# A gated linear attention block: the output gate's second half as two groups of 512 columns, three of its pair-steps by sums, and transposes and loads at later seams

## The chip, the cores and the metric

The kernel runs on one core of one Trainium2 chip. The metric is the device time of one execution in microseconds, as the median of several runs. PE is the matrix engine, DVE the vector engine, ACT the scalar engine, POOL the GpSimd engine and SP the engine that issues most DMAs. Every engine works through its own instructions in order.

## The reference

One layer: a chunked gated linear attention (GLA) with an output gate and an output projection, and an MLP with squared ReLU, each with RMSNorm ahead and a residual; 256 tokens of width 2048, in float32.

```python
def _gla_mixer(h, w_in, w_gate_up, b_gate, o_norm, w_out):
    proj = h @ w_in
    q, k, v, r, g_low = jnp.split(proj, [...], axis=-1)
    log_a = jax.nn.log_sigmoid((g_low @ w_gate_up + b_gate)) / GLA_GATE_TEMP
    ...
    _, o = lax.scan(step, s0, (qc, k_dec, vc, chunk_decay))
    o = o * lax.rsqrt(jnp.mean(o * o, axis=-1, keepdims=True) + EPS) * o_norm
    o = o.transpose(1, 0, 3, 2, 4).reshape(bsz, seq, GLA_VAL_WIDTH)
    return (o * jax.nn.silu(r)) @ w_out
...
    x = x + mixer(rmsnorm(x))
    x = x + (relu(rmsnorm(x) @ w_up) ** 2) @ w_down
```

The change touches the last part of the mixer: `r` (2048 columns of `proj`), its product with `o`, and the projection by `w_out` (2048 x 2048).

## The kernel before

Products are made in split float32: each factor is a high part (a cast to the matrix engine's rounded float32, on ACT) and a low part (the rest, on DVE), and three products of parts (high·high, high·low, low·high) stand for one. So each block of weights that arrives by DMA costs a cast on ACT (line 123) and a subtraction on DVE (line 136) before PE can use it.

The tokens are two row blocks of 128 (`NT`). The width is cut into 16 blocks of 128 rows of weights (kt), and in most places two of them make a pair-step (kp, 0 to 7) of 256 rows by 512 columns. `group` (line 294) runs eight such pair-steps for one group of 512 columns. A plain pair-step is 24 matmuls of 256 columns. A pair-step "by sums" (kp in `summed`) forms sums of blocks of weights and of inputs, as in Strassen's scheme, and needs 21: 9 in its own step and 12, `pending`, after the next step's matmuls. For that it loads its weights in two DMAs of 256 KB, adds one block onto another with an accumulating DMA that POOL issues (line 335) once the loads have landed, lets DVE make the sums (lines 233 and 234), and casts and splits a second slot (lines 363 and 365). After the last step by sums `combine` joins the sum banks.

Weights go through rings. `raw` has six buffers (and one "more"); the cast parts, `hi` and `lo`, have five slots, so the cast of the k-th slot waits until PE is done with the (k-5)th. A pair-step by sums takes two slots.

The order of the instructions on each engine is set by a scheduler that follows the program's order and its dependences; `tc.issue_after` puts an instruction behind another one in time, and `between[step]` runs side work (turns, loads, bank copies) at a seam, after the step's matmuls.

The stages around the change:

- `x_group(n, ...)` (line 731) runs `group` on columns of `w_in`: two groups of v (`V0`, `V1`), then two groups of r, the first half of the output gate (`G0`, `G1`), with the attention's heads (`attend`, line 781) at the seams. `gate_x` (line 801) takes Silu on ACT (line 803) and multiplies `on`, the attention's output, on DVE (line 804).
- The second half of the gate (1024 columns) goes through `natural` (line 183) instead: 16 steps of 128 rows by 1024 columns, 24 matmuls each, no sums. At its seams stand `side` jobs: after the third step turns 0 and 1, later four loads of `h` (the residual, `load_h`) and the copy of `h` into out group 0's banks (`begin_out(0)`). One job makes sums of `w_out` in advance and stores them (`make_sums`, lines 242 to 262). At the end `gate_out` (line 818) takes four Silus and four products.
- `turn` (line 839) transposes 512 columns of `on` on PE in 8 matmuls (line 845), and ACT and DVE put the result into `oth`/`otl` as high and low parts, or, for the kp in `FORMED`, as the input's sums (`turn_pair`, line 829, through the tiles `some` and `form`, lines 834 to 837). Turn q serves kp 2q and 2q+1.
- `out_group(g, ...)` (line 920) runs `group` on `w_out` for 512 output columns, g = 0 to 3, in the orders of `ORDER`. Turns 2 and 3 stand in out group 0 at step 1.

Of the kernel before, what the change touches and what calls it, by code (L numbers as in the profile page):

```python
# [29 lines left out]
AF = mybir.ActivationFunctionType  # L30
# [11 lines left out]
KEYW = HEADS * DK  # L42
# [27 lines left out]
def tile_gla_mlp(ctx, tc, x, xt, cols, w_vg, w_in, w_gate, w_out, w_up, w_down, final_norm, out):  # L70
# [14 lines left out]
    def psum_bank(i, name="acc"):  # L85
        return psum.tile([P, 512], F32, tag=f"b{i}", name=name)
# [21 lines left out]
    def flush():  # L108
        while side:
            side.popleft()()  # L110
# [272 lines left out]
    def rows(w, c0, n=G, r0=0):  # L383
        return lambda kt: w[r0 + kt * P : r0 + (kt + 1) * P, c0 : c0 + n]
# [122 lines left out]
    def load_h(t, half):  # L507
        h[t, half] = shared.tile([P, G], F32, tag=f"h{2 * half + t}", name="h")
        with tc.issue_after(last_load[0].ins):
            nc.sync.dma_start(out=h.get((t, half)), in_=x[t * P : (t + 1) * P, half * G : (half + 1) * G])  # L510
# [217 lines left out]
        scores(hd)  # L728
        scores(hd + 1, spare)

    def x_group(n, c0, order, summed, between, put, rows_of={}):

        def combine(p16, p57):
            tt = nc.vector.tensor_tensor
            nc.scalar.copy(comb_x[:, 1::2], two(p16))
            nc.scalar.copy(comb_x[:, 0::2], two(p57))
            tt(comb_x[:, 3], comb_x[:, 1], comb_x[:, 3], op=ALU.add)
            tt(comb_x[:, 0], comb_x[:, 0], comb_x[:, 3], op=ALU.subtract)
            tt(comb_x[:, 3], comb_x[:, 3], comb_x[:, 2], op=ALU.add)
            tt(comb_x[:, 2], comb_x[:, 0], comb_x[:, 2], op=ALU.subtract)  # L740

        def put_all(banks):
            for t in range(NT):
                o = comb_x[:, 2 * t : 2 * t + 2]
                nc.vector.tensor_tensor(o, two(banks[t]), o, op=ALU.add)
                put(o.rearrange("p f s -> p (f s)"), t)

        def at_of(kp):
            def at(k):
                if k < A12:  # L750
                    return [x_forms[kp][:, i, k] for i in range(2)]
                t, i = divmod((A11, A12, A21, A22).index(k), 2)
                return plain_x(2 * kp + i, t)
            return at

        def row(kt, t):
            return (row_x if (kt, t) in [(2 * kp + i, t) for kp in rows_of for t, i in rows_of[kp][:1]] else plain_x)(kt, t)

        group(
            lambda kp: w_in[2 * kp * P : 2 * (kp + 1) * P, c0 : c0 + GT], [psum_bank(i) for i in x_banks[n % 2]], x_sums,  # L760
            order, summed, between, row, at_of, combine, put_all, filled=False, rows_of=rows_of,
        )

    V0 = (5, 6, 2, 0, 7, 3, 4, 1), (0, 4)
# [41 lines left out]

    x_group(2, 4 * KEYW, *G0, {i + 1: f for i, f in enumerate(attends[:6])}, gate_x(0), {2: FIRST[2]})
    x_group(3, 4 * KEYW + GT, *G1, {i: f for i, f in enumerate(attends[6:])}, gate_x(GT), {2: FIRST[2]})
    acc_free.clear()
    acc_free.extend(x_banks[0] + x_sums + x_banks[1])  # L810
    jobs.extend(next(make))


    oth = otl = None

    some = mid.tile([P, 7, 512], F32, tag="qt", name="some")

    def gate_out(acc, c0):
        for c in range(2):
            for t in range(NT):  # L820
                lo = c0 + 512 * c
                s = some[:, 2 * c + t]
                nc.scalar.activation(s, acc[t][c], AF.Silu, scale=r1[:, t : t + 1])
                nc.vector.tensor_tensor(on[:, t, lo : lo + 512], on[:, t, lo : lo + 512], s, op=ALU.mult)

    FORMED = (0, 1, 6, 7)
    raw_forms = [in_forms(some[:, 4:6].rearrange("p a b -> p (a b)")), in_forms(mid.tile([P, G], F32, tag="db", name="form"))]
# [30 lines left out]
                nc.scalar.activation(dh, s, AF.Copy, scale=gain(kt))  # L858
                nc.vector.scalar_tensor_tensor(dl, s, gain(kt), dh.bitcast(F32), op0=ALU.mult, op1=ALU.subtract)

    once_x = lambda kt, t: (plain_x if kt == EVEN[1] else row_x)(kt, t)
    oth, otl = (big.tile([P, KT * T + 192], F32R, tag="B", name="ot" + i) for i in "hl")

    of_pairs = big.tile([P, 4 * G + 64], F32R, tag="C", name="of")[:, OFF:-16].rearrange("p (b i f s) -> p b i f s", b=2, i=2, f=8)
# [31 lines left out]
    def begin_out(g):  # L896

        for t in range(NT):
            out_banks[g, t] = bank = psum_bank(out_ids[2 * (g % 2) + t])
            nc.scalar.copy(bank, h[:, t, g * GT : (g + 1) * GT])  # L900

    def spare_out(g):
        return [psum_bank(out_ids[2 * (1 - g % 2) + t], "aux") for t in range(NT)]

    side.extend([nothing] * 2 + [lambda: (
        turn(on, turned_o, gain_o, 0, forms_o),
        turn(on, turned_o, gain_o, 1, forms_o, [psum_bank(i, "aux") for i in r_banks[4:]]),
    )])
    side.extend([nothing] + [lambda i=i: load_h(i % 2, i // 2) for i in range(4)] + [nothing] * 2 + [lambda: begin_out(0)])
    r_banks = list(acc_free)  # L910
    out_ids = r_banks[4:] + r_banks[:4]
    acc = natural(once_x, rows(w_in, 5 * KEYW), G, HALF, order=even_at(3, 5))
    flush()
    gate_out(acc, G)
    hs = const.tile([P, NT, 4], F32, name="hs")

    GROUPS = D // GT
# [27 lines left out]
    def ssq_h(g):  # L945
# [1 line left out]
            sq = tmp.tile([P, GT], F32, tag="t512", name="sq", bufs=1)  # L947
            nc.scalar.activation(sq, h[:, t, g * GT : (g + 1) * GT], AF.Square, accum_out=hs[:, t, g : g + 1])

    ORDER = (3, 0, 2, 1, 4, 7, 6, 5), (1, 3, 7, 2, 0, 6, 4, 5)  # L950
    newest[0] = None
    ordered[0] = True
    out_group(0, ORDER[0], FORMED, {
        1: lambda: (turn(on, turned_o, gain_o, 2), turn(on, turned_o, gain_o, 3, forms_o, spare_out(0))),
        3: lambda: begin_out(1),
    })
    hth, htl = (big.tile([P, KT, T], F32R, tag="A" + i, name="h" + i, bufs=1) for i in "hl")
    turned_h = lambda kt: [a[:, kt, :].rearrange("p (t s) -> p t s", t=NT) for a in (hth, htl)]
    for g in range(1, GROUPS):
        out_group(g, ORDER[1], FORMED if g == 3 else (0, 1, 7), {  # L960
            2: lambda: turn(h, turned_h, g2, g - 1), 4: lambda: ssq_h(g - 1),
            **({3: lambda: begin_out(g + 1)} if g + 1 < GROUPS else {}),
        })
# [511 lines left out]
```

## Time and profile before

| | |
|---|---|
| median of 3 runs | 1040.26 us (1039.97 to 1040.44) |
| the profiled execution | 1040.35 us |
| its span, first to last instruction | 1038.6 us |
| granted clock of PE | 0.998 |
| the second half of the gate, on PE | 238.78 to 284.12 us |
| turns 0 and 1 / turns 2 and 3, begin on PE | 246.94 us / 287.87 us |
| out group 0, begin on PE | 284.12 us |
| kp 7 of out group 0, begin on PE | 298.87 us |

Times count from the span's first instruction. In rows of the profile `L305` is line 305 of the program, `hi<-raw` is output from input by the tiles' names, `128x1024` partitions by elements, `x3` a count; a bracket holds the idle time of the engine ahead of the row and what ended it. A row of the timeline begins with start and duration, a row of the groups holds busy time and mean nanoseconds of one instruction behind the bar, then idle time by what ended it. A row of the chain begins with start and length. A row of the waits is waiter, releaser, total, count and longest.

### The profile page before, as it was taken

What the parts mean: (1) busy time and instruction counts of PE and PEld (TensorE: products, weight loads), DVE (VectorE), ACT (ScalarE), POOL (GpSimd) and SP (SyncE); (2) the same over time, 40 slices, a digit from 0 to 9 for tenths busy, and PEclk for the clock granted to TensorE, in tenths of its full rate; (3) what the DMA queues carried; (4) which work ended last, traced back from release to release, by engine and by line L of the source; (5) the groups of instructions that cost most, each with busy time, mean ns of one, the idle gap of its engine ahead of it and who ended that gap; (6) DMA issues with size and microseconds to landing.
All of it is one profiled execution on the core that took longest, in us unless ns stands there. A gap on an engine that the chain in (4) does not pass through costs nothing.

```text
span 1038.6 us, 23383 instructions
## 1 busy us (share of the span) xinstructions
PE 1029.9 (99%) x9016; PEld 1029.3 (99%) x9016; DVE 905.8 (87%) x1257; ACT 755.1 (73%) x1132; POOL 135.0 (13%) x181
## 2 busy tenths in 40 slices
PE   9999999999999999999999999999999999999997
PEld 9999999999999999999999999999999999999997
DVE  7769768898697876989999999999999999999987
ACT  7775556676576664678779788778778778778785
POOL 0000111310100001111111111111111111111100
PEclk9999999999999999999999999999999999999999
DMA  9967877758877877678888888887887888887872
GB/s 342 328 196 218 264 203 213 207 153 309 257 234 246 249 256 196 185 209 240 225 242 227 231 237 221 241 238 220 251 226 216 252 227 229 239 235 217 238 246 85
DMA packets 128751, 240.17 MB, mean 231 GB/s; under 512 B 11472, under 2 KB 30160, under 8 KB 128512
## 3 DMA queue, kind: packets, MB, share of 16 engines
q1 hardware_dynamic: 107472, 215.32, 65.8%
q0 software_dynamic: 20448, 21.77, 12.3%
q8 instruction: 70, 1.15, 0.4%
q10 hardware_dynamic: 720, 1.60, 0.4%
q14 instruction: 41, 0.34, 0.1%
HBM read 232.35 MB, written 6.29 MB: 230 GB/s over the span
## 4 chain that ended last, share of the span: by engine, by line
PE 98%; issue 0%; DMA 0%; ACT 0%; DVE 0%; POOLq 0%; POOL 0%; DVEq 0%; SPq 0%
PE up L1023 34%; PE acc L1023 28%; PE acc L305 16%; PE acc L181 10%; PE acc L224 6%; PE aux L224 2%; PE aux L181 1%; PE aux L845 1%; PE aux L696 1%; DMA raw<-in_w_vg 0%; ACT sqf L1362 0%; PE acc L595 0%; DVE hf L1434 0%; ACT hi L123 0%; POOLq L1471 0%
## 5 line engine op out<-in xcount | busy, mean ns | idle before, releaser
L123 ACT CAST hi<-raw 128x512 fp32r<-128x512 f32 (+4 forms) x656 | 519.0, 821 | 199.6 <-DVE raw L233 66.5
L136 DVE TENSOR_TENSOR lo<-raw,hi 128x768 fp32r<-128x768 f32 (+4 forms) x228 | 233.4, 1032 | 55.9 <-ACT hi L123 49.5
L1023 PE MATMUL acc<-hi,act 128*128 128x256 f32 x1694 | 247.6, 276 | 0.0
L1023 PE MATMUL up<-hh,hi 128*128 128x256 f32 x1024 | 238.7, 276 | 0.0
L1023 PE MATMUL up<-hl,hi 128*128 128x256 f32 x1024 | 238.7, 276 | 0.0
L1023 PEld LDWEIGHTS acc<-hi,act 128*128 128x128 f32 x1694 | 217.4, 188 | 0.0
L170 DVE TENSOR_TENSOR lo<-raw,hi 128x1024 fp32r<-128x1024 f32 x160 | 194.4, 1219 | 21.1 <-ACT hi L123 20.6
L1023 PEld LDWEIGHTS up<-hh,hi 128*128 128x128 f32 x1024 | 192.2, 188 | 0.0
L1023 PEld LDWEIGHTS up<-hl,hi 128*128 128x128 f32 x1024 | 192.2, 188 | 0.0
L1233 POOL DMA_DIRECT2D raw<-in_w_down x113 | 96.9, 857 | 518.1 <-DMA raw<-in_w_down 223.0
L1293 DVE TENSOR_TENSOR lo<-raw,hi 128x1024 fp32r<-128x1024 f32 x113 | 137.7, 1218 | 1.1 <-ACT hi L123 1.1
L1023 PE MATMUL up<-hh,lo 128*128 128x256 f32 x1024 | 137.0, 276 | 0.0
L1023 PE MATMUL acc<-lo,act 128*128 128x256 f32 x847 | 133.9, 276 | 0.0
L1023 PEld LDWEIGHTS up<-hh,lo 128*128 128x128 f32 x1024 | 125.7, 188 | 0.0
L1023 PEld LDWEIGHTS acc<-lo,act 128*128 128x128 f32 x847 | 113.3, 188 | 0.0
L234 DVE TENSOR_TENSOR raw<-raw 128x512 f32<-128x512 f32 x138 | 95.2, 690 | 3.4
L233 DVE TENSOR_TENSOR raw<-raw 128x256 f32<-128x256 f32 x138 | 58.3, 422 | 11.1 <-DMA raw<-in_w_out 8.0
L181 PE MATMUL acc<-hi,xA 128*128 128x256 f32 (+1 forms) x376 | 55.6, 280 | 0.2 <-ACT hi L123 0.2
L181 PEld LDWEIGHTS acc<-hi,xA 128*128 128x128 f32 x376 | 49.3, 188 | 0.4 <-ACT hi L123 0.4
L224 PE MATMUL acc<-xA,hi 128*128 128x256 f32 x288 | 49.2, 276 | 0.0
L1150 ACT COPY sums<-acc 128x512 f32<-128x512 f32 x46 | 26.9, 585 | 22.9 <-PE acc L1023 22.8
L224 PEld LDWEIGHTS acc<-xA,hi 128*128 128x128 f32 x288 | 43.5, 188 | 0.0
(226 smaller groups left out, 1443.1 us busy)
## 6 DMA issues: line engine op xcount, KB each, us to landing
raw<-in_w_up SPq DMA_DIRECT2D x128, 512.0 KB, 4.6
raw<-in_w_down SPq DMA_DIRECT2D x226, 256.0 KB, 4.5
raw<-in_w_in SPq DMA_DIRECT2D x69, 512.0 KB, 4.7
raw<-in_w_down POOLq DMA_DIRECT2D x113, 128.0 KB, 5.1
raw<-in_w_out SPq DMA_DIRECT2D x22, 512.0 KB, 6.2
raw<-in_w_down SPq DMA_DIRECT2D x15, 512.0 KB, 5.2
raw<-in_w_vg SPq DMA_DIRECT2D x14, 520.0 KB, 8.4
raw<-in_w_out SPq DMA_DIRECT2D x24, 256.0 KB, 5.4
```

The source lines that it names most:

```text
L123: last_hi[0] = nc.scalar.copy(to, raw)
L136: last_lo[0] = nc.vector.tensor_tensor(lo[:, s], raw[:, s], hi[:, s].bitcast(F32), op=ALU.subtract)
L170: last_lo[0] = nc.vector.tensor_tensor(to[1], dst, to[0].bitcast(F32), op=ALU.subtract)
L181: newest[0] = nc.tensor.matmul(o[:, m], x, w[:, m], start=first and c == 0, stop=last, skip_group_check=True).ins
L224: nc.tensor.matmul(o, u[:, i, s], m, start=kt == 0 and n == 0 and j % 2 == 0, stop=kt == KT - 1 and n == 2, skip_group_check=True,)
L233: nc.vector.tensor_tensor(u[:, 2], u[:, 0], u[:, 2], op=ALU.subtract)
L234: return nc.vector.tensor_tensor(u[:, 1::2], u[:, 1::2], u[:, 2:3].to_broadcast([P, 2, T]), op=ALU.subtract)
L305: newest[0] = nc.tensor.matmul(bank[:, o + d : o + d + T], x, w[:, d : d + T], start=(not filled or bank in sums_banks) and bank.name not ...
L1023: newest[0] = nc.tensor.matmul(o, x, w, start=first, stop=last, skip_group_check=True).ins
L1150: last_end[0] = nc.scalar.copy(to, src).ins
L1233: nc.gpsimd.dma_start(out=raw[:, :T], in_=src[:, 0, T:], accum_op=ALU.add)
L1293: last_lo[0] = nc.vector.tensor_tensor(to[1][:, :G], u, to[0][:, :G].bitcast(F32), op=ALU.subtract)
```

## The change

The second half of the gate is done by `x_group` twice (`G2` with three pair-steps by sums, `G3` with none), 512 columns each. `G2` ends with `gate_x`, `G3` with the new `gate_plain` (Silu on ACT at line 819 and the product on DVE at line 820 of the changed program, straight from the banks). Turns 0 and 1 stand after `G2`'s third step, turn 2 after `G3`'s third, turn 3 after out group 0's third step. Of the four loads of `h` two stand in `G3` and two in out group 0; `begin_out(0)` and the job that makes sums of `w_out` stand in `G3`. The order of out group 0 exchanges kp 2 and kp 1. Out group 2 has four pair-steps by sums, no longer three.

```diff
--- before.py
+++ after.py
@@ -728,7 +728,7 @@
         scores(hd)
         scores(hd + 1, spare)
 
-    def x_group(n, c0, order, summed, between, put, rows_of={}):
+    def x_group(n, c0, order, summed, between, put, rows_of={}, plain_put=None):
 
         def combine(p16, p57):
             tt = nc.vector.tensor_tensor
@@ -758,7 +758,7 @@
 
         group(
             lambda kp: w_in[2 * kp * P : 2 * (kp + 1) * P, c0 : c0 + GT], [psum_bank(i) for i in x_banks[n % 2]], x_sums,
-            order, summed, between, row, at_of, combine, put_all, filled=False, rows_of=rows_of,
+            order, summed, between, row, at_of, combine, plain_put or put_all, filled=False, rows_of=rows_of,
         )
 
     V0 = (5, 6, 2, 0, 7, 3, 4, 1), (0, 4)
@@ -806,22 +806,19 @@
 
     x_group(2, 4 * KEYW, *G0, {i + 1: f for i, f in enumerate(attends[:6])}, gate_x(0), {2: FIRST[2]})
     x_group(3, 4 * KEYW + GT, *G1, {i: f for i, f in enumerate(attends[6:])}, gate_x(GT), {2: FIRST[2]})
-    acc_free.clear()
-    acc_free.extend(x_banks[0] + x_sums + x_banks[1])
-    jobs.extend(next(make))
-
+    now = next(make)
 
     oth = otl = None
 
     some = mid.tile([P, 7, 512], F32, tag="qt", name="some")
 
-    def gate_out(acc, c0):
-        for c in range(2):
+    def gate_plain(c0):
+        def put(banks):
             for t in range(NT):
-                lo = c0 + 512 * c
-                s = some[:, 2 * c + t]
-                nc.scalar.activation(s, acc[t][c], AF.Silu, scale=r1[:, t : t + 1])
-                nc.vector.tensor_tensor(on[:, t, lo : lo + 512], on[:, t, lo : lo + 512], s, op=ALU.mult)
+                s = some[:, t]
+                nc.scalar.activation(s, banks[t], AF.Silu, scale=r1[:, t : t + 1])
+                nc.vector.tensor_tensor(on[:, t, c0 : c0 + GT], on[:, t, c0 : c0 + GT], s, op=ALU.mult)
+        return put
 
     FORMED = (0, 1, 6, 7)
     raw_forms = [in_forms(some[:, 4:6].rearrange("p a b -> p (a b)")), in_forms(mid.tile([P, G], F32, tag="db", name="form"))]
@@ -858,7 +855,6 @@
                 nc.scalar.activation(dh, s, AF.Copy, scale=gain(kt))
                 nc.vector.scalar_tensor_tensor(dl, s, gain(kt), dh.bitcast(F32), op0=ALU.mult, op1=ALU.subtract)
 
-    once_x = lambda kt, t: (plain_x if kt == EVEN[1] else row_x)(kt, t)
     oth, otl = (big.tile([P, KT * T + 192], F32R, tag="B", name="ot" + i) for i in "hl")
 
     of_pairs = big.tile([P, 4 * G + 64], F32R, tag="C", name="of")[:, OFF:-16].rearrange("p (b i f s) -> p b i f s", b=2, i=2, f=8)
@@ -902,16 +898,20 @@
     def spare_out(g):
         return [psum_bank(out_ids[2 * (1 - g % 2) + t], "aux") for t in range(NT)]
 
-    side.extend([nothing] * 2 + [lambda: (
-        turn(on, turned_o, gain_o, 0, forms_o),
-        turn(on, turned_o, gain_o, 1, forms_o, [psum_bank(i, "aux") for i in r_banks[4:]]),
-    )])
-    side.extend([nothing] + [lambda i=i: load_h(i % 2, i // 2) for i in range(4)] + [nothing] * 2 + [lambda: begin_out(0)])
-    r_banks = list(acc_free)
-    out_ids = r_banks[4:] + r_banks[:4]
-    acc = natural(once_x, rows(w_in, 5 * KEYW), G, HALF, order=even_at(3, 5))
-    flush()
-    gate_out(acc, G)
+    out_ids = x_banks[0] + x_banks[1] + x_sums
+    two_turns = lambda q, ids: (
+        turn(on, turned_o, gain_o, q, forms_o),
+        turn(on, turned_o, gain_o, q + 1, forms_o, [psum_bank(i, "aux") for i in ids]),
+    )
+    G2 = (5, 0, 4, 2, 3, 1, 6, 7), (0, 4, 1)
+    G3 = (0, 1, 5, 2, 4, 3, 6, 7), ()
+    x_group(4, 5 * KEYW, *G2, {2: lambda: two_turns(0, x_banks[1])}, gate_x(G), {2: FIRST[2]})
+    x_group(5, 5 * KEYW + GT, *G3, {
+        0: lambda: load_h(0, 0), 1: lambda: (now[10](), load_h(1, 0)),
+        2: lambda: (now[11](), turn(on, turned_o, gain_o, 2)), 5: lambda: begin_out(0),
+    }, None, {2: FIRST[2]}, gate_plain(G + GT))
+    acc_free.clear()
+    acc_free.extend(out_ids)
     hs = const.tile([P, NT, 4], F32, name="hs")
 
     GROUPS = D // GT
@@ -947,17 +947,17 @@
             sq = tmp.tile([P, GT], F32, tag="t512", name="sq", bufs=1)
             nc.scalar.activation(sq, h[:, t, g * GT : (g + 1) * GT], AF.Square, accum_out=hs[:, t, g : g + 1])
 
-    ORDER = (3, 0, 2, 1, 4, 7, 6, 5), (1, 3, 7, 2, 0, 6, 4, 5)
+    ORDER = (3, 0, 1, 2, 4, 7, 6, 5), (1, 3, 7, 2, 0, 6, 4, 5)
     newest[0] = None
     ordered[0] = True
     out_group(0, ORDER[0], FORMED, {
-        1: lambda: (turn(on, turned_o, gain_o, 2), turn(on, turned_o, gain_o, 3, forms_o, spare_out(0))),
+        2: lambda: turn(on, turned_o, gain_o, 3, forms_o), 4: lambda: load_h(0, 1), 5: lambda: load_h(1, 1),
         3: lambda: begin_out(1),
     })
     hth, htl = (big.tile([P, KT, T], F32R, tag="A" + i, name="h" + i, bufs=1) for i in "hl")
     turned_h = lambda kt: [a[:, kt, :].rearrange("p (t s) -> p t s", t=NT) for a in (hth, htl)]
     for g in range(1, GROUPS):
-        out_group(g, ORDER[1], FORMED if g == 3 else (0, 1, 7), {
+        out_group(g, ORDER[1], FORMED if g >= 2 else (0, 1, 7), {
             2: lambda: turn(h, turned_h, g2, g - 1), 4: lambda: ssq_h(g - 1),
             **({3: lambda: begin_out(g + 1)} if g + 1 < GROUPS else {}),
         })
```

How it shows in the order of the engines, at three places. Numbers behind a tile's name tell buffers apart. First DVE, from the loads ahead of the gate's second half to the first turns (`comb` is the result of gate group `G1`, `on` the gated output that the turns read; lines 737 to 745 join the sum banks, line 804 is the gate's product). Before:

```order
L136 TENSOR_TENSOR lo_3202<-raw_3203,hi_3201 128x1024
L136 TENSOR_TENSOR lo_3232<-raw_3233,hi_3231 128x1024
L136 TENSOR_TENSOR lo_3304<-raw_3305,hi_3303 128x1024
L737 TENSOR_TENSOR comb_1834<-comb_1834 128x256
L738 TENSOR_TENSOR comb_1834<-comb_1834 128x256
L739 TENSOR_TENSOR comb_1834<-comb_1834 128x256
L740 TENSOR_TENSOR comb_1834<-comb_1834 128x256
L136 TENSOR_TENSOR lo_3334<-raw_3335,hi_3333 128x1024
L745 TENSOR_TENSOR comb_1834<-acc_2854,comb_1834 128x512
L745 TENSOR_TENSOR comb_1834<-acc_2855,comb_1834 128x512
L136 TENSOR_TENSOR lo_3366<-raw_3367,hi_3365 128x1024
L804 TENSOR_TENSOR on_2477<-on_2477,comb_1834 128x512 x2
```

With the change (`raw_3199` and `raw_3220` are the weights of `G2`'s first two steps by sums):

```order
L234 TENSOR_TENSOR raw_3220<-raw_3220 128x2x256
L365 TENSOR_TENSOR lo_3240<-raw_3199,hi_3239 128x1024
L739 TENSOR_TENSOR comb_1834<-comb_1834 128x256
L136 TENSOR_TENSOR lo_3301<-raw_3298,hi_3300 128x1024
L740 TENSOR_TENSOR comb_1834<-comb_1834 128x256
L745 TENSOR_TENSOR comb_1834<-acc_2854,comb_1834 128x512
L745 TENSOR_TENSOR comb_1834<-acc_2855,comb_1834 128x512
L365 TENSOR_TENSOR lo_3329<-raw_3220,hi_3328 128x1024
L136 TENSOR_TENSOR lo_3348<-raw_3345,hi_3347 128x1024
L804 TENSOR_TENSOR on_2477<-on_2477,comb_1834 128x512
L136 TENSOR_TENSOR lo_3380<-raw_3375,hi_3379 128x768
L804 TENSOR_TENSOR on_2477<-on_2477,comb_1834 128x512
```

Between the first line 739 row and the last line 804 there stood two subtractions of line 136, of 1024 elements each; now there are two of 1024 and one of 768, and one of line 365 (`lo_3329`, the sums of `raw_3220`). Ahead of that row stand the rest of the two steps by sums, of which the piece shows the last two rows.

Second POOL, from the attention's last norms on (`ors` is the inverse root that the attention's result waits for). Before, the rows of `ors_2897` and `ors_2938` follow each other. With the change:

```order
L335 DMA raw_3054<-in_w_in 128x256
L521 TENSOR_TENSOR ors_2753<-oss_2749,mhalf_101 128x1
L521 TENSOR_TENSOR ors_2792<-oss_2788,mhalf_101 128x1
L521 TENSOR_TENSOR ors_2897<-oss_2893,mhalf_101 128x1
L335 DMA raw_3199<-in_w_in 128x256
L335 DMA raw_3220<-in_w_in 128x256
L521 TENSOR_TENSOR ors_2938<-oss_2934,mhalf_101 128x1
L335 DMA raw_3375<-in_w_in 128x256
```

Two accumulating DMAs of `G2`'s loads stand between the attention's last two norms.

Third ACT, in out group 0 around the last turn (`some` and `form` are the two tiles of the turn's sums for kp 6 and 7, rows `oth<-some` and `oth<-form` their cast; line 900 before and line 896 after is `begin_out(1)`). Before:

```order
L834 ACTIVATE some_3162<-aux_3794,colt_81 128x2x128 x2
L834 ACTIVATE form_3163<-aux_3795,colt_81 128x2x128 x2
L123 CAST hi_3918<-raw_3865 128x2x256
L858 ACTIVATE oth_3164<-aux_3776,colt_81 128x256
L900 COPY acc_3884<-h_3363 128x512
L858 ACTIVATE oth_3164<-aux_3777,colt_81 128x256
L900 COPY acc_3886<-h_3395 128x512
L836 CAST oth_3164<-some_3162 128x1024
L123 CAST hi_3939<-raw_3935 128x768
L836 CAST oth_3164<-form_3163 128x1024
L123 CAST hi_3958<-raw_3954 128x768
L123 CAST hi_3973<-raw_3935 128x2x256 x2
```

With the change:

```order
L896 COPY acc_3925<-h_3515 128x512
L896 COPY acc_3927<-h_3556 128x512
L123 CAST hi_3931<-raw_3929 128x1024
L123 CAST hi_3965<-raw_3961 128x768
L123 CAST hi_3986<-raw_3982 128x768
L831 ACTIVATE some_3162<-aux_3854,colt_81 128x2x128 x2
L831 ACTIVATE form_3163<-aux_3855,colt_81 128x2x128 x2
L123 CAST hi_4001<-raw_3961 128x2x256 x2
L123 CAST hi_4020<-raw_4018 128x1024
L833 CAST oth_3164<-some_3162 128x1024
L833 CAST oth_3164<-form_3163 128x1024
```

The first casts of kp 7 and kp 6 (`hi_3939` and `hi_3958` before) stood behind the turn's copies, and the cast of kp 7's sums (`hi_3973`) behind the casts of the turn's sums. Now the casts of kp 4, 7 and 6 (`hi_3931`, `hi_3965`, `hi_3986`) stand ahead of the turn's first row, and those of kp 7's sums and of kp 5 (`hi_4001`, `hi_4020`) between the turn's copies and the casts of its sums. `begin_out(1)` moved from behind the copies to ahead of all of them.

## The prediction

> **What bounds the kernel now.** I read the page first: the busy times and the chain that ended last.
>
> ```profile
> span 1038.6 us, 23383 instructions
> PE 1029.9 (99%) x9016; PEld 1029.3 (99%) x9016; DVE 905.8 (87%) x1257; ACT 755.1 (73%) x1132; POOL 135.0 (13%) x181
> PE 98%; issue 0%; DMA 0%; ACT 0%; DVE 0%; POOLq 0%; POOL 0%; DVEq 0%; SPq 0%
> ```
>
> PE is busy for 99 % and the end hangs on it for 98 %. A matmul less shortens the span, and any wait of PE lengthens it one for one. DVE at 87 % is close behind. The view of waits on PE has only two rows, both in the first 5 us:
>
> ```profile
> PE aux L399 <- DVE ones L396: 1.1, 1, 1.1
> PE acc L181 <- ACT hi L123: 0.2, 1, 0.2
> ```
>
> So no wait can be removed, and the question is what the change takes from PE and what new waits it makes. The price of a matmul comes from the chain in order of time, around the edit:
>
> ```profile
> 221.94 17.00 PE acc L305 x150
> 238.94 8.17 PE acc L181 x72
> 248.85 35.43 PE acc L181 x312
> ```
>
> 17.00/150, 8.17/72 and 35.43/312 are 113.3, 113.5 and 113.6 ns for a matmul of 256 columns.
>
> **The change part by part: what PE saves.** A plain pair-step is 24 matmuls, one by sums 21. The second half of the output gate was 16 steps of 24 (72 + 312 = 384); it becomes eight plain pair-steps, five plain ones and three by sums, 384 − 9. The output projection's third group gets one more by sums, −3. The transposes stay 32. Hence 12 × 0.113 = **−1.36 us**. The third group's new step by sums costs DVE 1.8 us more (0.87 + 0.34 + 0.60 at the pitches below, and an L365), two casts and a DMA:
>
> ```profile
> L233 DVE TENSOR_TENSOR raw<-raw 128x256 f32<-128x256 f32 x17 | 7.2, 421 | 4.6 <-DMA raw<-in_w_out 4.3
> ```
>
> In the stretch around these groups (170 to 345 us) DVE idles 4.3 us ahead of L233 alone, on loads of `w_out`; that covers it. I price it at nothing, and at 1.8 us if that cover is gone.
>
> **Wait A: the first turns.** They need the gated output of group 3 (`gate_x(GT)`, L804). How it goes today:
>
> ```profile
> 238.78 0.62 PE L181 MATMUL acc<-hi,xA 128*128 128x256 f32 x4
> 246.94 1.91 PE L845 MATMUL aux<-ident,on 128*128 128x128 f32 x16
> 228.85 0.42 DVE L233 TENSOR_TENSOR raw<-raw 128x256 f32<-128x256 f32 x1
> 229.31 0.69 DVE L234 TENSOR_TENSOR raw<-raw 128x512 f32<-128x512 f32 x1
> 230.69 1.23 DVE L365 TENSOR_TENSOR lo<-raw,hi 128x1024 fp32r<-128x1024 f32 x1 [0.69 <-PE acc L305]
> 231.83 3.49 DVE L136 TENSOR_TENSOR lo<-raw,hi 128x1024 fp32r<-128x1024 f32 x3
> 241.00 1.28 DVE L745 TENSOR_TENSOR comb<-acc,comb 128x512 f32<-128x512 f32 x2
> 243.93 1.29 DVE L804 TENSOR_TENSOR on<-on,comb 128x512 f32<-128x512 f32 x2
> ```
>
> The last L804 ends at 243.93 + 1.29 = 245.22, and the transposes begin at 246.94, after 72 matmuls: 1.7 us of margin. In the changed kernel the turns stand after 24 + 9 + 9 + 12 = 54 matmuls, so PE reaches them at 238.78 + 54 × 0.1133 = 244.90. The first eight transposes (columns 0 to 511, long ready) take 8 × 1.91/16, less the overlap, about 0.83: at 245.73 PE wants the L804s.
>
> They come later than today, since the next group's steps by sums stand ahead of them on DVE. Back to back, an instruction starts 0.08 us before the one ahead is recorded as ended (three of 1.22 make 3.49), so a pitch is the duration less 0.08: 1.14 for an L365 or a 1024 L136, 0.60 for L234, L745 and L804 (1.28 and 1.29 for two), 0.34 for L233 (0.42). Two groups of DVE give the rest:
>
> ```profile
> L136 DVE TENSOR_TENSOR lo<-raw,hi 128x768 fp32r<-128x768 f32 x19 | 18.1, 953 | 1.4 <-ACT hi L123 1.3
> L737 DVE TENSOR_TENSOR comb<-comb 128x256 f32<-128x256 f32 x4 | 1.7, 420 | 0.0
> ```
>
> 0.87 for a 768 L136, 0.34 for each of L737 to L740. I count from the L233 of group 3's last step by sums, at 228.85 today; I set it 0.47 later (0.3 to 1.3), at 229.3. The attention's last L521 on POOL, on which the DVE work just ahead of it waits, now stands behind two accumulating DMAs (L335), which wait for their loads:
>
> ```profile
> 207.29 0.80 SPq L334 DMA_DIRECT2D raw<-in_w_in  x2
> 210.69 0.88 POOL L335 DMA_DIRECT2D raw<-in_w_in  x1 [3.02 <-DVE oss L794]
> 221.03 0.34 SPq L173 DMA_DIRECT2D raw<-in_w_in  x1
> 222.77 0.33 SPq L173 DMA_DIRECT2D raw<-in_w_in  x1
> 224.87 0.55 POOL L521 TENSOR_TENSOR ors<-oss,mhalf 128x1 f32<-128x1 f32 x1 [1.72 <-DVE oss L794]
> ```
>
> An L335 starts some 3 us after its loads' issue (210.69 against 207.29). The loads of the two new steps take the places issued at 221.03 and 222.77, so the second L335 starts near 226.2 and the L521 near 226.8, not 224.87.
>
> From 229.3 DVE has: L233, L234 and the wait behind them 1.84 (228.85 to 230.69); three L365 3.42; four 1024 L136 4.56; three 768 L136 2.61; two L233 and two L234 1.88; L737 to L740 1.36; two L745 1.20; one L804 0.60 and the last at its full 0.69. That is 18.2, so the last L804 ends at about 247.45, and PE waits 247.45 − 245.73 = **1.7 us**; I take 1.6, as the transposes of the first row block can run ahead.
>
> A bound from below that leaves DVE's backlog out: the sixth load's cast (768 columns) stands between the two Silus on ACT and needs the slot that PE frees after 42 matmuls, at 243.5. The fifth's cast ends near 243.5, the first Silu at 244.2, the sixth's cast at 244.9; DVE then has the fifth's lo to 244.6, an L804 to 245.2, the sixth's lo to 246.1 and the L804 to 246.7. So A is at least 1.0; with the late L521 at its worst it is 2.6.
>
> **Wait B: the last turn.** Turn 3 (forms of kp 7 and 6) moves from out group 0's step 1 to its step 2, kp 7 stays at step 5.
>
> ```profile
> 284.12 0.39 PE L305 MATMUL acc<-hi,oth 128*128 128x256 f32 x2
> 287.87 1.91 PE L845 MATMUL aux<-ident,on 128*128 128x128 f32 x16
> 298.87 0.39 PE L305 MATMUL acc<-hi,oth 128*128 128x256 f32 x2
> 293.10 1.08 ACT L836 CAST oth<-some 128x1024 fp32r<-128x1024 f32 x1
> 294.78 1.08 ACT L836 CAST oth<-form 128x1024 fp32r<-128x1024 f32 x1
> 296.23 1.22 DVE L837 TENSOR_TENSOR otl<-form,oth 128x1024 fp32r<-128x1024 f32 x1
> ```
>
> Today kp 7's first matmul comes at 298.87, 81 matmuls behind the transposes; its form's low part ends at 297.45, 1.4 us ahead. Now call T the begin of out group 0 (284.12 in the first row). The turn follows 54 matmuls, T + 6.1 to T + 7.0; then 24 + 12 + 24 = 60 matmuls, so PE wants the form at T + 13.8 and its low part at T + 14.1.
>
> DVE and ACT get there later. ACT casts kp 1's sums when a slot comes free after 24 matmuls (T + 2.7, done T + 4.0), copies two banks (`begin_out(1)`), casts kp 4, 7 and 6 by T + 8.0; DVE's low part of kp 6 ends at T + 9.0. The form's operations were ahead of such casts, now they are behind. Then DVE has ten small ones in a row, 3.4 together (two steps' L233 and L234, 1.88; six of the forms, below), and only when eight of these are done, at T + 11.0, can ACT cast kp 7's sums (1.3), kp 5 (0.95), `some` (1.0) and `form` (1.1): T + 15.5. DVE meanwhile: L365, kp 5's lo, `some`, `form`, 4 × 1.14 from T + 12.4, ending at T + 17.0.
>
> ```profile
> 290.48 0.28 DVE L835 TENSOR_TENSOR some<-some 128x128 f32<-128x128 f32 x1
> 290.88 0.42 DVE L835 TENSOR_TENSOR some<-some 128x256 f32<-128x256 f32 x1
> 286.86 1.71 ACT L123 CAST hi<-raw 128x1024 fp32r<-128x1024 f32 x2 [0.77 <-ACT hi L123]
> 297.86 0.62 ACT L123 CAST hi<-raw 128x512 fp32r<-128x512 f32 x1 [1.26 <-PE acc L305]
> ```
>
> Six at 0.20, 0.34 and 0.20 twice are 1.5. PE waits 17.0 − 14.1 = **2.85 us**. From below: if only the slots paced ACT (kp 5's slot comes free at T + 11.0), casts and lows would end at T + 15.5, a wait of 1.3. From above, half a microsecond of further lag: 3.2.
>
> **Pace after a stall.** After its turns PE runs a stretch slower, 0.40 us for two matmuls where it has 0.39, with a step at 302.72:
>
> ```profile
> 302.72 0.42 PE L305 MATMUL acc<-lo,oth 128*128 128x256 f32 x2
> 302.98 0.40 PE L305 MATMUL acc<-hi,oth 128*128 128x256 f32 x2
> 303.21 0.40 PE L305 MATMUL acc<-hi,otl 128*128 128x256 f32 x2
> ```
>
> The starts lie 0.236 apart there against 0.227, 4.5 ns a matmul. Two waits set that pace for about 20 matmuls more than today: +0.1 us, between nothing and 0.5.
>
> **Sum.** −1.36 + 1.6 + 2.85 + 0.1 = +3.2. The profiled run took 1040.35 (span 1038.6 and 1.75 around it), the median of the runs is 1040.26, so 1040.26 + 3.2 = **1043.4 us**.
>
> **Rivals.** (1) *Only one wait*. Both have the same root, DVE's queue, but A rests on the order at a seam that is full today and B on ACT's order in out group 0. With only A the sum is +0.3, with only B +1.6, and with that one at its bound from below −0.4 (A) or −0.1 (B): 1039.9 to 1041.9. For it: today both places have margin (1.7 and 1.4 us). Against: even the bounds from the slots alone leave both waits standing. (2) *Not slower: neither wait*, the saving stands alone, 1040.26 − 1.36 = 1038.9. It decides by whether L804 ends before 245.73 and the form's low part before T + 14.1. That would need DVE or ACT to finish 1.0 and 1.3 us earlier than the slots allow. (3) *A third wait*: DVE leaves the first turns late and carries it into the next steps by sums; 0.5 to 2 us more, up to 1045.5. Against: 24 plain matmuls behind the turns, 2.7 us, give it back. (4) *The clock closes in wait B*. PE's first sixteen matmuls ran slow, 3.40 us where sixteen transposes of the same shape take 1.91; the rest of the span shows nothing of it, but no wait either:
>
> ```profile
> 1.05 3.40 PE L399 MATMUL aux<-ones 128*128 128x128 f32 x16 [1.05 <-DVE ones L396]
> PEclk9999999999999999999999999999999999999999
> ```
>
> If a wait of 2.85 us brought such a start back, it would add 3.40 − 1.91 = 1.5 us: 1044.9.
>
> The Trainium skill ("TensorE: Matmul & The Clock Gate", part 1, the HAM clock gate) has PE fall to half its clock after an idle window of about 3.4 us, and need as long a busy one to come back. By that rule wait B is just short of it; if it were caught, some 1.7 us would come on top, an estimate from that page. No row of the profile before shows PE idle that long behind its start.
>
> **Chances.** Both waits between their bounds (−1.36 + 1.0 + 1.3 to −1.36 + 2.6 + 3.2 + 0.5: 1041.2 to 1045.2): 0.70, with 1043.4 the likeliest. Only one: 0.15. Neither: 0.07. A third wait 0.05, the clock 0.03. The range leaves out the case of neither, the outer parts of (3) and (4) and some of the low end of (1): **1040.4 to 1045.0**. A measurement of this kernel tells about 0.2 % from no change, 2.08 us. Slower than 1042.34: most of the first case (0.52) and the last two, 0.60. Between 1038.18 and 1042.34: 0.37. Faster than that, only as a part of the case of neither wait, with a saving I don't see: 0.03.
>
> **What would show it.** PE's waits must have two new rows: a transpose at L842 on DVE's `on` (1.0 to 2.6 us, about 245 us into the span) and a matmul at L305 on `otl` or `oth` of DVE or ACT (1.3 to 3.2 us, about 14 us into out group 0). PE's count must be 9004. If the count is right and both rows are missing, I misread the queues of DVE and ACT; if the rows are there with another size, a slot or L521 was mis-sized; a wait elsewhere on PE would mean that a seam I took to have margin has none.

## The result, and the profile after

The changed kernel took 1048.13 us (median of 6 runs, 1045.70 to 1051.17), the kernel before 1040.12 us (6 runs, 1039.81 to 1041.67). The ratio is 1.0079, with a 95 % interval from 1.0068 to 1.0091: slower, by more than was forecast (1043.4, range to 1045.0). Its runs also spread over 5.5 us, where those of the kernel before agree within 1.9.

The profiled execution took 1047.07 us. Its page, and below it all rows of the waits on PE:

```profile
span 1045.3 us, 23422 instructions
PE 1030.4 (99%) x9004; PEld 1029.1 (98%) x9004; DVE 915.9 (88%) x1275; ACT 760.2 (73%) x1142; POOL 139.1 (13%) x185
PEclk9999999999999999999999999999999999999999
```

```profile
PE aux L842 <- DVE on L804: 2.7, 2, 1.8
PE acc L305 <- DVE otl L834: 1.9, 1, 1.9
PE aux L399 <- DVE ones L396: 1.1, 1, 1.1
PE acc L305 <- ACT oth L833: 0.7, 1, 0.7
PE acc L181 <- ACT hi L123: 0.2, 1, 0.2
```

PE has its 12 matmuls fewer (9004), yet its busy time rose from 1029.9 to 1030.4 us: some matmuls took longer. The two waits that were forecast are there and are the only new ones. PE's row of the timeline (start, duration) shows their sizes and a third thing:

```profile
244.09 1.04 PE L842 MATMUL aux<-ident,on 128*128 128x128 f32 x8
246.90 0.41 PE L842 MATMUL aux<-ident,on 128*128 128x128 f32 x2 [1.77 <-DVE on L804]
248.28 0.88 PE L842 MATMUL aux<-ident,on 128*128 128x128 f32 x6 [0.97 <-DVE on L804]
248.91 0.48 PE L305 MATMUL acc<-hi,xe_gt 128*128 128x256 f32 x2
...
286.32 0.39 PE L305 MATMUL acc<-hi,oth 128*128 128x256 f32 x2
...
301.04 0.50 PE L305 MATMUL acc<-hi,oth 128*128 128x256 f32 x2 [0.68 <-ACT oth L833]
303.42 0.51 PE L305 MATMUL acc<-hi,otl 128*128 128x256 f32 x2 [1.88 <-DVE otl L834]
304.00 0.62 PE L305 MATMUL acc<-lo,oth 128*128 128x256 f32 x3
304.42 0.42 PE L305 MATMUL acc<-hi,oth 128*128 128x256 f32 x1
...
307.77 0.28 PE L305 MATMUL acc<-hi,otl 128*128 128x256 f32 x1
```

The sixteen first transposes take from 244.09 to 248.91, 4.82 us, against 1.67 before: wait A cost 3.15 us. Out group 0 begins at 286.32, and the pair on `otl`, reckoned for 14.1 us behind that, is due at 300.4 and comes at 303.42: wait B cost 3.0 us. Then, from 304.2 to 307.7, a single matmul takes 0.42 us instead of 0.28. The clock says why. The view of windows gives busy time and count by engine, then PE's granted clock:

```profile
246.22:249.63 3.41, 1.76 (x14) 1.56 (x15) 3.41 (x6) 2.39 (x7) 0.00 (x0) 1.00 0.90 293
249.63:253.04 3.41, 3.41 (x32) 3.41 (x32) 3.41 (x10) 2.30 (x6) 0.00 (x0) 1.00 0.94 308
300.83:304.24 3.41, 1.32 (x9) 1.12 (x10) 3.41 (x4) 1.24 (x4) 0.87 (x1) 1.00 1.02 400
304.24:307.65 3.41, 3.41 (x19) 3.41 (x18) 1.85 (x3) 1.84 (x2) 0.36 (x1) 0.50 1.07 347
307.65:311.06 3.41, 3.41 (x30) 3.41 (x30) 2.63 (x4) 0.83 (x1) 0.51 (x1) 1.00 1.01 313
```

PE ran at half clock for 3.41 us right behind wait B. The page's row PEclk can't show it: a digit covers 26 us. At 113 ns a matmul the 17 matmuls from 304.24 to 307.77 would have taken 1.93 us and took 3.53: 1.6 us.

So the profiled execution adds up: −1.36 for the matmuls, +3.15, +3.0, +1.6, and nothing worth a term for the pace: +6.4, of 6.7 measured. The rest is two differences that have nothing to do with the change. The third gate group began 0.8 us earlier in this execution (237.97, before 238.78); about 0.5 us of that is a stretch of 116 matmuls from 203.0 us on, which started 117.8 ns apart in the profile before and 113.7 in this one. And the last output's DMA landed 0.9 us later behind PE's last matmul.

The median of the six runs lies another 1.06 us above the profiled execution; no trace of those runs was kept.

### The profile page after: what moved, and what is told of

The parts are those of the page before. It is cut to its first block, busy times and chain, and to the rows that moved or that the text cites. A ratio compares the mean times of both kernels' runs of the same rounds, so it can differ in the third digit from the quotient of the medians.

```text
span 1045.3 us, 23422 instructions
## 1 busy us (share of the span) xinstructions
PE 1030.4 (99%) x9004; PEld 1029.1 (98%) x9004; DVE 915.9 (88%) x1275; ACT 760.2 (73%) x1142; POOL 139.1 (13%) x185
## 4 chain that ended last, share of the span: by engine, by line
PE 70%; issue 0%; ACT 0%; DVE 0%; POOLq 0%; POOL 0%; DVEq 0%
PE up L1023 33%; PE acc L1023 28%; PE acc L305 7%; PE acc L181 2%; PE aux L842 0%; ACT sqf L1362 0%; DVE hf L1434 0%; POOLq L1471 0%; POOL rf L521 0%; PE row L986 0%; DVEq L1471 0%; DVE sf L1423 0%; ACT h L1150 0%
## 5 line engine op out<-in xcount | busy, mean ns | idle before, releaser
L1023 PEld LDWEIGHTS acc<-lo,act 128*128 128x128 f32 x847 | 113.3, 188 | 0.0
L234 DVE TENSOR_TENSOR raw<-raw 128x512 f32<-128x512 f32 x142 | 98.0, 690 | 3.5
L233 DVE TENSOR_TENSOR raw<-raw 128x256 f32<-128x256 f32 x142 | 60.0, 422 | 9.5 <-DMA raw<-in_w_out 6.5
L305 PE MATMUL acc<-hi,xA 128*128 128x256 f32 x408 | 64.2, 276 | 0.0
L305 PEld LDWEIGHTS acc<-hi,xA 128*128 128x128 f32 x408 | 54.6, 188 | 0.0
```

The lines of the kernel that those rows point to most:

```text
L233: nc.vector.tensor_tensor(u[:, 2], u[:, 0], u[:, 2], op=ALU.subtract)
L234: return nc.vector.tensor_tensor(u[:, 1::2], u[:, 1::2], u[:, 2:3].to_broadcast([P, 2, T]), op=ALU.subtract)
L305: newest[0] = nc.tensor.matmul(bank[:, o + d : o + d + T], x, w[:, d : d + T], start=(not filled or bank in sums_banks) and bank.name not ...
L1023: newest[0] = nc.tensor.matmul(o, x, w, start=first, stop=last, skip_group_check=True).ins
```

## The experiments

Each kernel was run beside the kernel before on the same chip; each entry gives both medians.

**Taking wait B away.** Out group 0 gets its old order back, and turn 3 stands a step earlier.

```diff
-    ORDER = (3, 0, 1, 2, 4, 7, 6, 5), (1, 3, 7, 2, 0, 6, 4, 5)
+    ORDER = (3, 0, 2, 1, 4, 7, 6, 5), (1, 3, 7, 2, 0, 6, 4, 5)
...
-        2: lambda: turn(on, turned_o, gain_o, 3, forms_o), 4: lambda: load_h(0, 1), 5: lambda: load_h(1, 1),
+        1: lambda: turn(on, turned_o, gain_o, 3, forms_o), 4: lambda: load_h(0, 1), 5: lambda: load_h(1, 1),
```

> The changed kernel with wait B taken away: out group 0 in its old order (3, 0, 2, 1, ...) and turn 3 after its second step, so that 81 matmuls instead of 60 lie between the turn and kp 7; the first turns stay late. Theory (two waits of PE, 3.15 us at the first turns and 3.0 us at kp 7, and PE at half clock for a window of 3.4 us, 1.6 us, behind the second): kp 7's wait goes or falls under 0.5 us, the slow window with it, and the runs come to the changed kernel's lowest run less 3.0, 1042.7 us, within 1 us of each other. Rival (the clock's dip has nothing to do with kp 7's wait, or the spread of the runs, 1045.7 to 1051.2, comes from loads): a slow window is still there or the runs still spread over 3 us or more, around 1045. Second rival (turn 3 now waits for the gate's last product, line 820): a new wait at the turn, up to 1 us, 1043.5.

1045.34 us (1042.10 to 1045.73, 5 runs), before 1040.15. Waits on PE, and the windows around the first turns:

```profile
PE aux L842 <- DVE on L804: 2.7, 2, 1.7
PE aux L399 <- DVE ones L396: 1.1, 1, 1.1
```

```profile
245.51:248.92 3.41, 1.42 (x12) 0.98 (x10) 3.41 (x5) 3.41 (x7) 0.00 (x0) 1.00 0.87 253
248.92:252.33 3.41, 2.74 (x13) 2.74 (x14) 3.41 (x9) 1.66 (x4) 0.00 (x0) 0.50 0.98 363
```

Wait B is gone and no wait took its place at the turn; the lowest run, 1042.10, is where the theory put all of them. But the slow window did not go: it now stands behind wait A, which left the clock alone in the changed kernel's profile. The same wait closes the clock in one execution and not in another. That part of the expectation was wrong, and the rival, by which the slow window is not kp 7's alone and the runs spread over 3 us or more (they spread over 3.6), was right in so far that wait A can bring it too.

**Taking wait A away.** Turns 0 and 1 stand one step later in the third gate group.

```diff
-    G2 = (5, 0, 4, 2, 3, 1, 6, 7), (0, 4, 1)
+    G2 = (5, 0, 4, 3, 2, 1, 6, 7), (0, 4, 1)
...
-    x_group(4, 5 * KEYW, *G2, {2: lambda: two_turns(0, x_banks[1])}, gate_x(G), {2: FIRST[2]})
+    x_group(4, 5 * KEYW, *G2, {3: lambda: two_turns(0, x_banks[1])}, gate_x(G), {2: FIRST[2]})
```

> The changed kernel with wait A taken away: turns 0 and 1 stand one step later in the gate's third group (kp 2 and 3 exchanged so that kp 2 still follows the turns), 24 matmuls or 2.7 us later for PE; kp 7's wait stays. Theory: the wait at the transposes falls from 3.15 us to 0.4 or less, kp 7's wait stays at about 3.0 us and the clock closes behind it in most runs: 1042.9 us where it does not close, 1044.5 where it does once. Rival (the queue of DVE is late by a fixed amount, so the wait only moves): the transposes still wait 2 us or more, and the runs stay at 1045.7 to 1048.

1046.42 us (1043.92 to 1046.62, 5 runs), before 1040.15.

```profile
PE acc L305 <- DVE otl L834: 1.9, 1, 1.9
PE aux L842 <- DVE on L804: 1.6, 2, 1.4
PE acc L305 <- ACT oth L833: 0.7, 1, 0.7
```

```profile
299.12:302.53 3.41, 1.30 (x10) 0.90 (x8) 3.41 (x4) 2.49 (x4) 0.00 (x0) 1.00 1.00 371
302.53:305.94 3.41, 2.93 (x13) 2.93 (x14) 2.37 (x3) 0.83 (x1) 0.87 (x1) 0.50 1.05 375
268.40:271.81 3.41, 1.82 (x15) 1.39 (x14) 3.41 (x5) 3.41 (x6) 0.55 (x1) 1.00 0.88 284
```

The first turns no longer wait, wait B is as it was and closes the clock behind it. But the row on line 842 is now another turn: turn 2 in the fourth group, at 270.9 us, waits for the third group's product. Half of wait A had moved on, as the rival said, and the median lies in the rival's range (1045.7 to 1048), not where the theory put it (1042.9 or 1044.5).

**Both edits at once.**

> Both moves at once: all that the change takes from PE (12 matmuls, 1.36 us) and neither wait. Theory: 1040.1 - 1.4 = 1038.8 us, or 1039.6 with a remainder of 0.4 us at each place, no slow window, runs within 1 us of each other. Rival (other costs of the change that the two waits hide, such as the transposes in three places, or the pace after a stall): 1041 or more, with the cost at a third place of PE.

1040.95 us (1040.05 to 1041.63, 11 runs), before 1040.15; ratio 1.0007 (0.9999 to 1.0016). PE's one new wait of size is turn 2's:

```profile
PE aux L842 <- DVE on L804: 1.4, 2, 1.2
```

No window ran at half clock in its profile, and the spread fell from 5.5 to 1.6 us. Seven of the eight us that the change had cost are back; turn 2's wait eats the 1.36 us that the matmuls save. The theory, 1038.8 to 1039.6 us, was missed: the rival's cost at a third place is there. Saving and wait cancel, so they do not account for the 0.8 us between the two medians, which the interval does not tell from nothing.

**The third output group's step alone**, on the kernel before: `FORMED if g >= 2` for `FORMED if g == 3`.

> The kernel before with one part of the change alone: the output projection's third group with four pair-steps by sums. Theory (three matmuls less, DVE's idle time covers its work): 0.34 us faster, 1039.8 us, no new row among PE's waits. Rival (DVE's 1.8 us more work is not covered): a new wait of PE in that group, 1040.1 to 1041.6 us.

1039.73 us (1039.27 to 1041.18, 11 runs), before 1040.15; ratio 0.9999 (0.9990 to 1.0008). No new wait on PE. The medians differ by 0.42 us, the ratio by 0.1 us; the interval holds the 0.34 us of three matmuls and no change as well, so only the missing wait is shown.

**Turn 2 one step later as well.**

```diff
-    G3 = (0, 1, 5, 2, 4, 3, 6, 7), ()
+    G3 = (0, 1, 5, 4, 2, 3, 6, 7), ()
...
-        2: lambda: (now[11](), turn(on, turned_o, gain_o, 2)), 5: lambda: begin_out(0),
+        2: now[11], 3: lambda: turn(on, turned_o, gain_o, 2), 5: lambda: begin_out(0),
```

> The kernel with both waits taken away, and turn 2 one step later in the gate's fourth group too (kp 2 and 4 exchanged), since the transposes of turn 2 waited 1.2 to 1.4 us there for the gate's product (line 804). Theory (that wait is the whole remainder): it goes, PE has no wait left but the start's, and the runs come to 1040.95 - 1.4 = 1039.5 us, with a lowest under 1039.0. Rival (DVE is behind by its total work in these two groups, and the wait only moves on): a wait of 0.5 us or more appears later, at kp 4 or in out group 0, and the median stays at 1040.5 or more.

1042.15 us (1041.14 to 1044.31, 9 runs), before 1040.16: its median is higher than with turn 2 in its place (1040.95).

```profile
PE aux L842 <- DVE on L820: 1.6, 2, 1.4
```

Line 820 is the fourth group's product: now turn 3 waits. The rival was right. Each of these moves of a turn handed DVE's work to the next seam. The wait is only 0.2 us longer than turn 2's was, so most of the 1.2 us between the two medians is not explained by it; two of the nine runs, 1043.84 and 1044.31 us, had a mean clock of 0.996.

**The inverse root ahead of the DMAs.** Line 521's last row on POOL is put ahead of the third group's accumulating DMAs, in the kernel with turn 3 early. Nothing else moves; the wait that remains is A.

```diff
-                nc.gpsimd.dma_start(out=raw[:, :T], in_=src[:, 0, T:], accum_op=ALU.add)
+                with ExitStack() as first:
+                    if norms_first[0]:
+                        first.enter_context(tc.issue_after(last_rs[0]))
+                    nc.gpsimd.dma_start(out=raw[:, :T], in_=src[:, 0, T:], accum_op=ALU.add)
...
-        nc.gpsimd.tensor_tensor(dst, ms, mhalf, op=ALU.pow)
+        last_rs[0] = nc.gpsimd.tensor_tensor(dst, ms, mhalf, op=ALU.pow).ins
...
+    norms_first[0] = True
     x_group(4, 5 * KEYW, *G2, {2: lambda: two_turns(0, x_banks[1])}, gate_x(G), {2: FIRST[2]})
+    norms_first[0] = False
```

> The kernel with turn 3 early (kp 7's wait gone, 2.7 us left at the first turns), with one thing more: on POOL the attention's last inverse root (line 521, now 525) is put ahead of the accumulating DMAs of the gate's third group; nothing else is moved. Theory (half of wait A is the inverse root standing behind these DMAs: it ended at 227.98, and DVE's multiplication waited 1.6 us for it): DVE's queue runs about 1.6 us earlier, the transposes wait 1.0 to 1.6 us in all, no window idles 1.9 us, the clock stays up: 1040.5 to 1041.5 us, spread under 1.5 us. Rival (the sums on DVE alone make wait A): the wait stays at 2.3 us or more, slow windows in some runs, 1045 median.

1041.74 us (1039.65 to 1042.38, 11 runs), before 1040.16. The kernel without this edit took 1045.34. First the changed kernel's timeline (POOL, then DVE), then this one's, with line numbers one to four higher:

```profile
224.52 0.92 POOL L335 DMA_DIRECT2D raw<-in_w_in  x1 [2.05 <-DMA raw<-in_w_in]
226.53 0.88 POOL L335 DMA_DIRECT2D raw<-in_w_in  x1 [1.09 <-DVE lo L136]
227.09 0.89 POOL L521 TENSOR_TENSOR ors<-oss,mhalf 128x1 f32<-128x1 f32 x1
...
228.02 0.81 DVE L797 TENSOR_SCALAR on<-aux,r1k,ors 128x512 f32<-128x512 f32 x1 [1.62 <-POOL ors L521]
229.88 0.42 DVE L233 TENSOR_TENSOR raw<-raw 128x256 f32<-128x256 f32 x1
...
247.54 0.68 DVE L804 TENSOR_TENSOR on<-on,comb 128x512 f32<-128x512 f32 x1
```

```profile
224.99 0.55 POOL L525 TENSOR_TENSOR ors<-oss,mhalf 128x1 f32<-128x1 f32 x1 [1.72 <-DVE oss L798]
225.63 0.92 POOL L339 DMA_DIRECT2D raw<-in_w_in  x1
...
226.25 0.81 DVE L801 TENSOR_SCALAR on<-aux,r1k,ors 128x512 f32<-128x512 f32 x1
228.97 0.42 DVE L234 TENSOR_TENSOR raw<-raw 128x256 f32<-128x256 f32 x1
...
246.79 0.69 DVE L808 TENSOR_TENSOR on<-on,comb 128x512 f32<-128x512 f32 x1
```

```profile
PE aux L846 <- DVE on L808: 1.0, 1, 1.0
PE acc L306 <- DVE lo L137: 0.5, 1, 0.5
```

The multiplication no longer waits, and PE's wait at the first turns falls from 2.7 to 1.0 us, as the theory had it; no window closed in the profile. The median lies 0.2 us over the theory's range, and the runs spread over 2.7 us, not under 1.5. (PE reached these groups 0.9 us later than in the changed kernel's execution, so the starts compare only against PE's. Against the kernel that this one was edited from, DVE's last product ends 2.46 us behind PE's first transpose, 245.02 to 247.48, and there 4.05, 245.49 to 249.54: 1.6 us earlier.) The second row is new: 0.5 us in the third output group, at 344 us, on the added step by sums. The cover that I had claimed for it is thin.

**The inverse root ahead and the first turns late**, that is, this edit on the kernel with both waits taken away.

> The kernel with both waits taken away, with the inverse root ahead of the accumulating DMAs as well. Theory (turn 2's wait comes from DVE's queue, which is late from the seam ahead on): DVE runs earlier, the wait at turn 2 shrinks from 1.4 us by 0.5 to 1.4, 1039.5 to 1040.4 us. Rival (turn 2's wait is set by when PE ends the third group's last steps, that is by slots, not by a late start): the wait stays at 1.2 to 1.4 us, 1040.9.

1040.23 us (1039.54 to 1044.00, 11 runs), before 1040.16; ratio 1.0008 (0.9998 to 1.0017). Turn 2's wait fell from 1.4 to 0.8 us:

```profile
PE aux L846 <- DVE on L808: 0.8, 2, 0.6
```

About half of that wait came from DVE's late start, the other half did not. Three of the runs took 1041.90, 1043.26 and 1044.00 us at a mean clock of 0.998, as most of the others, so their extra time is not the clock's; what it is stays open.

**The third gate group plain**, with turn 3 early and the first turns where the change has them.

```diff
-    G2 = (5, 0, 4, 2, 3, 1, 6, 7), (0, 4, 1)
+    G2 = (5, 0, 4, 2, 3, 1, 6, 7), ()
...
-    x_group(4, 5 * KEYW, *G2, {2: lambda: two_turns(0, x_banks[1])}, gate_x(G), {2: FIRST[2]})
+    x_group(4, 5 * KEYW, *G2, {2: lambda: two_turns(0, x_banks[1])}, None, {2: FIRST[2]}, gate_plain(G))
```

> The kernel with turn 3 early, the gate's third group with no pair-step by sums and the first turns where the change has them (behind 72 matmuls again, as before the change). Theory (wait A is made by the sums: their work on DVE, the inverse root behind their DMAs, and the 18 matmuls fewer ahead of the turns): no wait at the first turns, 9 matmuls more (1.02 us): 1042.1 - 3.1 + 1.0 = 1040.0 us, no slow window. Rival (the two groups of 512 columns as such bring the wait, by their slots): a wait of 0.5 us or more at the first turns or at turn 2, 1040.5 to 1042.

1039.32 us (1038.63 to 1041.27, 11 runs), before 1040.16; ratio 0.9994 (0.9986 to 1.0003). PE waits nowhere but at the start:

```profile
PE aux L399 <- DVE ones L396: 1.1, 1, 1.1
```

Groups of 512 columns bring no wait as such; the sums do, by their work on DVE, by the inverse root behind their DMAs and by the 18 matmuls fewer ahead of the first turns. The run takes away all three at once and does not part them. It is the lowest median of all and 0.84 us under the kernel before, but the interval does not tell it from no change.

**Two steps by sums instead of three**, with everything that helped: `G2 = (5, 0, 4, 3, 2, 1, 6, 7), (0, 4)`.

> The kernel with both waits taken away and the inverse root ahead of the accumulating DMAs, with two pair-steps by sums (kp 0 and 4) in the gate's third group, no longer three: three matmuls more (0.34 us), 1.8 us less on DVE, and the sum banks are joined after kp 3 and no longer after kp 6. Theory (turn 2's last 0.6 to 0.8 us of wait come from DVE's work of the third step by sums and the late joining): no wait of PE left, 9 matmuls fewer than before (1.02 us), 1039.1 us or, without the slow stretch in out group 0, 1038.7; it would stand about 0.3 us under the kernel with the plain third group. Rival (DVE is short of time in these two groups even so): a wait at turn 2 or 3 of 0.5 us or more, 1039.8 to 1041.

1039.58 us (1038.65 to 1042.19, 11 runs), before 1040.22; ratio 0.9997 (0.9988 to 1.0007). The theory had no wait left. The wait at the turns is gone, but the wait in the third output group is there again:

```profile
PE acc L306 <- DVE lo L137: 0.5, 1, 0.5
```

No better than the plain group, though it has six matmuls fewer.

## Why the prediction was wrong, by its own steps

The sign and both places were right, and the sum was too small by 4.7 us against the median. Two terms failed. DVE's start ahead of wait A was mis-sized, and wait A cost 1.55 us more than its term; the clock, left out of the sum, cost 1.6 us in the profiled execution. Of the rest, wait B has 0.15 us and the profiled execution's own differences about 0.3; the 1.06 us by which the median lies above that execution stay open. With the two waits as measured, and no clock, the sum is 1045.05 us, already out of the range.

- **Matmuls, −1.36 us**: right (9004 of them).
- **Wait A, 1.6 us (1.0 to 2.6)**: the mechanism was right, the size was not; it cost 3.15. The term that was mis-sized is the start from which DVE's work was counted, "0.47 later (0.3 to 1.3)". DVE's work from that L233 to the last L804 took 18.34 us (229.88 to 248.22), reckoned 18.2. But the L233 stood 8.09 us ahead of the group's first matmul (237.97), reckoned 9.48. The inverse root ended at 227.98, and DVE stood idle for it for 1.62 us: it stood behind both accumulating DMAs, as I wrote, but it began 0.3 us later than reckoned (227.09, reckoned 226.8) and took 0.89 us, not 0.55, and PE reached the group 0.8 us earlier. Counted from PE's arrival, the root ended 9.99 us ahead, reckoned 11.43 (227.35 to 238.78). PE's early arrival is not the reason: in the kernel with turn 3 early PE came at 239.36, and the root still ended only 10.06 us ahead (229.30). The edit that puts the root ahead took 1.7 us off the wait; the 1.0 us left was gone where the third group had no sums and the turns their 72 matmuls ahead again.
- **Wait B, 2.85 us (1.3 to 3.2)**: right. From the group's begin (286.32) the form's low part was reckoned at 17.0 and PE's need at 14.1; the pair on `otl` started at 17.1. It cost 3.0, and it went when turn 3 moved.
- **The pace after a stall**, 0.1 us (up to 0.5): too small to matter in the changed kernel's profile, as reckoned. It is not always: with turn 3 early, 193 matmuls behind wait A started 117.8 ns apart, where 113.3 is usual, which is 0.9 us. Behind the 0.5 us wait in the third output group it was 109 matmuls, another 0.5 us, in each of the two profiles.
- **The clock**: this step failed as a mechanism. "The clock closes in wait B" stood among the rivals with 1.5 us and a chance of 0.03, since wait B alone lasts less than the 3.4 us of the rule in the Trainium skill ("TensorE: Matmul & The Clock Gate", part 1), by which a whole window must be idle. The trace differs from that rule, and the trace decides: windows in which PE was busy for 1.32, 1.42 and 1.30 of 3.41 us were followed by one at half clock, windows with 1.76 and 1.82 were not. Both waits are long enough to bring a window under the bound, or not, according to where the window's edge falls; wait A did so in one profile and not in another. The slow window took 1.6 us in the changed kernel's profile. The changed kernel's lowest run, 1045.70, comes near the sum without it (1040.26 − 1.36 + 3.15 + 3.0 = 1045.05); the profiled one had one such window. How many each of the slower runs had is not shown, since they left no trace. The profiles without such a window have a mean clock of 0.997 to 0.999, those with one 0.995 to 0.997, so the two highest runs (1051.17 at 0.994, 1050.11 at 0.995) had at least one. The runs at 1048.01 and 1048.26 read 0.997 like the profiled one and took 1 us more, so the clock is a part of the spread and not shown to be all of it.
- **"The third group's step at nothing"**: right in the changed kernel, and in the kernel with that step alone; in two other kernels PE waited 0.5 us there, with the slower pace behind it.
- **"A third wait", 0.05**: it did not come, but was one step away: with the first turns moved, turn 2 waited, and with turn 2 moved, turn 3.

What the change wanted, 12 matmuls less, can be had only as far as DVE has time: in these two groups it must make the sums, turn the attention's output and take the gate's product. With no sums in the third group the kernel has no wait, and three of the twelve matmuls.

## What to carry to other kernels

Where PE is the bound and DVE is close behind, a matmul saved by work on DVE is paid for at the next seam at which PE needs DVE's last result; count DVE's queue from the instruction that starts it, and look at what that one waits for on a third engine. In this kernel a wait of PE of two to three microseconds had to be priced with the chance that the clock drops behind it. And a turn moved away from its wait handed the wait to the next turn until work went with it.

## What the runs showed of the hardware

PE's clock fell to half when PE was busy for 38 to 42 % of the 3.41 us ahead (1.30 to 1.42 us), and not at 52 or 53 % (1.76 and 1.82). The end of the kernel, where PE runs out of work, narrows the bound. With the third gate group plain, a window with 1.58 us of PE's work, 46 %, left the clock up, and only the empty one behind it closed it; with the inverse root ahead, a window with 1.14 us closed it at once:

```profile
1027.92:1031.33 3.41, 1.58 (x14) 1.38 (x13) 2.94 (x12) 1.63 (x6) 0.55 (x1) 1.00 0.65 243
1031.33:1034.74 3.41, 0.00 (x0) 0.00 (x0) 0.87 (x3) 0.85 (x2) 0.00 (x0) 1.00 0.93 348
1034.74:1036.80 2.06, 0.00 (x0) 0.00 (x0) 0.00 (x0) 0.00 (x0) 0.00 (x0) 0.50 0.12 43
1031.13:1034.54 3.41, 1.14 (x11) 0.94 (x9) 2.94 (x11) 1.70 (x6) 0.55 (x1) 1.00 0.79 297
1034.54:1037.95 3.41, 0.00 (x0) 0.00 (x0) 0.43 (x2) 0.41 (x1) 0.00 (x0) 0.50 0.86 318
```

So in these profiles the bound lies where PE is busy for 42 to 46 % of a window, as the profile models its busy time. Inside the kernel the clock came back after one window, in which PE was busy for 2.74 to 3.41 us. The windows do not move with the wait: in the three profiles that had a slow window, the clock closed 300.37, 242.35 and 296.96 us after its first stretch at full speed began, which is 88, 71 and 87 times 3.413 us. So one and the same wait closes the clock in some executions only, and a spread of the runs that the kernel before does not have can be a sign of a wait near that bound. It need not be: three runs of one kernel here stood 2.4 to 4.5 us above its lowest with no sign of it in their clock.
